# Two pairs of FFN chunks per phase as seven block products each, and TensorE in the written order from the third chunk on

## The chip, the cores and the metric

One core of one Trainium2 chip. The metric is the device time of one execution in microseconds (us); lower is better.

## What is computed

Two layers of a streaming encoder on a sequence of 256 tokens with model width 1024, everything in float32. Each layer is a half-step FFN, a mixer (attention and mLSTM heads) and another half-step FFN, each between two RMS norms. The change touches the FFN:

```python
def _swiglu(h, w_in, w_out):
    gate, up = jnp.split(h @ w_in, 2, axis=-1)
    return (jax.nn.silu(gate) * up) @ w_out
...
h = _swiglu(_rmsnorm(x, g[0]), ffn_w_in[l, 0], ffn_w_out[l, 0])
x = x + 0.5 * _rmsnorm(h, g[1])
```

Here `w_in` is 1024 x 5632 (gate and up side by side, 2816 each) and `w_out` is 2816 x 1024. A phase reads 33 MB of FFN weights, and there are four FFN phases and two mixers.

## The kernel before

**Precision.** TensorE multiplies fp32r numbers. Every weight and every activation is therefore split into a rounded high part and a low rest, and every product is three matmuls: high by high, high by low, low by high (`mm3`, L401, L402, L403).

**Tiling.** The hidden width 2816 is cut into 11 chunks of 256 (`NC_FF`), the tokens into two tiles of 128 (`NT`). For one chunk the first product ("I" below) takes, for each token tile, the two K halves (512 rows each, `kh`) of 512 columns: 256 gate columns and 256 up columns side by side in one PSUM bank of 512. That is 2 weight pieces and 48 matmuls of 128x512. The second product ("O") takes the chunk's 256 hidden columns to the 1024 outputs: 1 weight piece and 24 matmuls, added up in four `bk` banks over all chunks.

**Weights.** A piece is 128x2048 float32, 1 MB, loaded by one DMA of SP's queue into a raw tile `wr` (3 buffers, L282). It is worked on in two halves of 128x1024. ScalarE (ACT) makes the high part `wh` (L288), VectorE (DVE) the low part `wl` by subtracting it (L289). Halves lie in 7 buffers each of `wl` and `wh`, and in each run of ten halves three more come from the pool `k4` (`half_tiles`). So a half can be cast only when TensorE (PE) has finished with the half ten places before it.

**Between the two products.** ACT takes silu of the gate (L266), DVE makes `h` (L528), ACT writes `h` as 16-bit planes (L535), a transposing DMA of SP's queue turns it (`turned`, L537), DVE copies it together again (`hT`, L539), and ACT and DVE split it into `hh` (L550) and `hl` (L551). The last chunk is computed with weights and tokens exchanged (`in_turned`, `ffn_turned`), so that it needs no turning.

**Order.** The Python code writes I of chunk c, then O two chunks behind (`DEFER`). The framework's scheduler then decides where each instruction stands in its engine's queue; only from "ending" on (the last chunk's end of a phase, up to "running" of the next) does PE follow the written order. Each engine works through its queue in that fixed order. PSUM has 2 `pin`, 2 `ptr` and 4 `bk` banks.

Of the kernel before, what the change touches and what calls it, by code (L numbers as in the profile page):

```python
# [59 lines left out]
def _pack(inp):  # L60
# [9 lines left out]
    def ffn(at, l, f):  # L70
        a = w_in[l, f].reshape(2, 4, P, 2, NC_FF, 256)
        a = a.transpose(4, 0, 2, 1, 3, 5).reshape(NC_FF, 2, P, 2048)
        b = w_out[l, f].reshape(NC_FF, 2, P, D).transpose(0, 2, 1, 3).reshape(NC_FF, P, 2048)
        order = [a[0, 0], a[0, 1]]
        for c in range(1, NC_FF):
            order += [a[c, 0], a[c, 1], b[c - 1]]
        for piece in order + [b[NC_FF - 1]]:
# [54 lines left out]
class _Trunk:  # L132
# [144 lines left out]
    def begin_piece(self):  # L277

        nc, i = self.nc, self.piece_at
# [3 lines left out]
        js = iter(range(2))  # L283

        def part():
            j = next(js)
            lo, hi = self.half_tiles(i, j)
            ia = nc.scalar.activation(hi, raw[:, j], AF.Copy)  # L288
            iv = nc.vector.tensor_tensor(lo, raw[:, j], hi.bitcast(F32), op=ALU.subtract)  # L289
            for oa, ov in self.turns.pop(0) if self.turns else ():  # L290
                self.after(ia, [oa] if oa else [])
                self.after(iv, [ov] if ov else [])
# [237 lines left out]
    def ffn_planes(self, h):  # L530
# [8 lines left out]
        nc.vector.tensor_copy(hT.rearrange("p b n -> p (b n)").bitcast(U16).rearrange("p (n u) -> p u n", u=2),  # L539
                              turned.rearrange("p (u b) n -> p u (b n)", u=2))  # L540
# [46 lines left out]
    def ffn(self, pre, gi_post):  # L587
# [30 lines left out]
        po, pend = None, []  # L618
        if not xT:
# [12 lines left out]
            h = self.t2("h", (P, NT, 256))  # L632
            for t in range(NT):
                self.ffn_hidden(pins[t], r[t], h[:, t])
            h = self.ffn_planes(h)
            begin = 1
        else:
# [24 lines left out]
            h = self.ffn_planes(h)  # L662
            begin = 2
        for c in range(begin, NC_FF):
# [5 lines left out]
            if c < TURN:  # L670
                pins = [self.bank_pin() if c % 2 else self.bank_tr() for _ in range(NT)]
                for kh in range(2):
                    for t in range(NT):
                        in_piece(t, kh, pins[t], ws[kh])
# [582 lines left out]
```

## Time and profile before

| | |
|---|---|
| median of 3 runs | 961.61 us (961.54 to 962.01) |
| the profiled execution | 962.02 us |
| its span in the profile | 960.2 us |
| mean granted TensorE clock | 0.999 |

In the profile PE is the matrix engine, PEld its weight load, DVE VectorE, ACT ScalarE, POOL GpSimd, and SP the engine whose queue issues the DMAs. A row such as "L289 DVE TENSOR_TENSOR wl<-wr,wh 128x1024 ... x324 | 389.2, 1221 | 180.4 <-ACT wh L288 174.4" says: 324 instructions of line 289, 389.2 us busy in all, 1221 ns each, and 180.4 us of idle time of DVE just before them, 174.4 of it ended by the ACT instruction that wrote `wh`. In a timeline a row gives start, duration, engine, line and operation, and "x2" joins two neighbours.

### The profile page before, as it was taken

Reading aid. Unit: us, or ns where it says so; the run is one execution under the profiler, and the core shown is the slowest. Engines: PE = TensorE matmul, PEld = TensorE weight load, DVE = VectorE, ACT = ScalarE, POOL = GpSimd, SP = SyncE. Lnnn points to the kernel's source line nnn. Section 1 sums busy time; section 2 is a strip of 40 time slices with the busy share of each in tenths; the row PEclk is TensorE's granted clock in tenths of the full one; section 3 lists DMA queues with packets and bytes.
Section 4 is the critical chain, followed back from the end, with each engine's and each line's share of the span. In section 5 each row is a group of like instructions: output and inputs, shape, how many; then the busy total and the mean of one; then the engine's idle time right before and its main releaser. Section 6 shows DMA issues by size and latency. Waiting matters only on the chain.

```text
span 960.2 us, 12037 instructions
## 1 busy us (share of the span) xinstructions
PE 952.8 (99%) x4523; PEld 788.9 (82%) x4523; DVE 638.7 (67%) x945; ACT 571.2 (59%) x937; POOL 29.5 (3%) x55
## 2 busy tenths in 40 slices
PE   9999999999999999999999999999999999999997
PEld 7888888888888888888888888888888888888885
DVE  6765655689867766555687555566988676755553
ACT  8755554577856655454476555555778466555542
POOL 2000000000010000000000000000001000000000
PEclk9999999999999999999999999999999999999999
DMA  8996656236352975676458666653454257765621
GB/s 317 328 288 202 225 193 219 105 132 241 116 192 91 299 245 193 218 247 176 154 189 283 206 225 208 196 187 128 172 202 174 90 182 256 272 205 192 225 72 44
DMA packets 69879, 189.32 MB, mean 197 GB/s; under 512 B 45274, under 2 KB 46426, under 8 KB 49086
## 3 DMA queue, kind: packets, MB, share of 16 engines
q1 hardware_dynamic: 69246, 187.95, 58.0%
q8 instruction: 35, 0.57, 0.2%
q10 hardware_dynamic: 576, 0.61, 0.2%
q14 instruction: 22, 0.18, 0.1%
HBM read 177.01 MB, written 1.05 MB: 185 GB/s over the span
## 4 chain that ended last, share of the span: by engine, by line
PE 97%; DVE 1%; DMA 1%; ACT 0%; issue 0%; POOLq 0%; DVEq 0%; ACTq 0%
PE pin L401 13%; PE pin L402 13%; PE pin L403 13%; PE bk L401 10%; PE bk L402 10%; PE bk L403 10%; PE ptr L402 6%; PE ptr L403 6%; PE ptr L401 6%; PE pin L610 1%; PE ptr L610 1%; PE ptr L879 1%; PE ptr L427 1%; DMA wr<-in_w_dram 1%; PE bk L1094 1%; PE ptr L615 1%
## 5 line engine op out<-in xcount | busy, mean ns | idle before, releaser
L289 DVE TENSOR_TENSOR wl<-wr,wh 128x1024 fp32r<-128x1024 f32 x324 | 389.2, 1221 | 180.4 <-ACT wh L288 174.4
L288 ACT ACTIVATE wh<-wr 128x1024 fp32r<-128x1024 f32 x324 | 333.9, 1055 | 171.2 <-DMA wr<-in_w_dram 44.1
L401 PE MATMUL pin<-wh,both 128*128 128x512 f32 x560 | 221.2, 396 | 0.0
L403 PE MATMUL pin<-wh,both 128*128 128x512 f32 x560 | 218.3, 390 | 0.0
L402 PE MATMUL pin<-wl,both 128*128 128x512 f32 x560 | 218.2, 390 | 0.0
L401 PE MATMUL bk<-wh,hh 128*128 128x512 f32 x352 | 137.4, 390 | 0.1
L402 PE MATMUL bk<-wl,hh 128*128 128x512 f32 x352 | 137.0, 389 | 0.0
L403 PE MATMUL bk<-wh,hl 128*128 128x512 f32 x352 | 136.9, 389 | 0.0
L403 PEld LDWEIGHTS pin<-wh,both 128*128 128x128 f32 x560 | 105.1, 188 | 22.3
L401 PEld LDWEIGHTS pin<-wh,both 128*128 128x128 f32 x560 | 105.3, 188 | 22.0 <-issue 0.7
L402 PEld LDWEIGHTS pin<-wl,both 128*128 128x128 f32 x560 | 105.3, 188 | 20.6
L403 PE MATMUL ptr<-wh,both 128*128 128x512 f32 x256 | 99.4, 389 | 0.0
L402 PE MATMUL ptr<-wl,both 128*128 128x512 f32 x256 | 99.4, 389 | 0.0
L401 PE MATMUL ptr<-wh,both 128*128 128x512 f32 x256 | 98.9, 389 | 0.0
L401 PEld LDWEIGHTS bk<-wh,hh 128*128 128x128 f32 x352 | 66.1, 188 | 14.0 <-ACT hh L550 0.5
L403 PEld LDWEIGHTS bk<-wh,hl 128*128 128x128 f32 x352 | 66.1, 188 | 13.7
L402 PEld LDWEIGHTS bk<-wl,hh 128*128 128x128 f32 x352 | 66.1, 188 | 13.5
L539 DVE COPY hT<-turned 128x1024 uint16<-128x1024 uint16 x40 | 30.3, 757 | 41.9 <-DMA turned<-planes 41.5
L401 PEld LDWEIGHTS ptr<-wh,both 128*128 128x128 f32 x256 | 48.1, 188 | 10.0
L402 PEld LDWEIGHTS ptr<-wl,both 128*128 128x128 f32 x256 | 48.1, 188 | 10.0
L550 ACT ACTIVATE hh<-hT 128x256 fp32r<-128x256 f32 x80 | 28.9, 409 | 46.0 <-DVE hT L539 46.0
L403 PEld LDWEIGHTS ptr<-wh,both 128*128 128x128 f32 x256 | 48.1, 188 | 9.9
(210 smaller groups left out, 891.9 us busy)
## 6 DMA issues: line engine op xcount, KB each, us to landing
wr<-in_w_dram SPq DMA_DIRECT2D x162, 1024.0 KB, 5.2
gpost<-in_gpost_dram SPq DMA_DIRECT2D x6, 512.0 KB, 6.3
wr<-in_w_dram SPq DMA_DIRECT2D x2, 512.0 KB, 6.1
wr<-in_w_dram SPq DMA_DIRECT2D x3, 256.0 KB, 4.3
x<-in_x_dram SPq DMA_DIRECT2D x3, 256.0 KB, 4.4
turned<-planes SPq DMA_TRANSPOSE x40, 4.4
out_dram<-x SPq DMA_DIRECT2D x2, 256.0 KB, 2.1
x<-in_x_dram SPq DMA_DIRECT2D x2, 128.0 KB, 3.0
```

Of the source, the lines that this page charges most:

```text
L288: ia = nc.scalar.activation(hi, raw[:, j], AF.Copy)
L289: iv = nc.vector.tensor_tensor(lo, raw[:, j], hi.bitcast(F32), op=ALU.subtract)
L401: mm(ps, xh, wh, start=start, stop=False)
L402: mm(ps, xh, wl, start=False, stop=False)
L403: mm(ps, xl, wh, start=False, stop=stop)
L427: nc.tensor.transpose(ptr[:, k, :], x[:, (4 * hf + k) * P:(4 * hf + k + 1) * P], self.ident)
L539: nc.vector.tensor_copy(hT.rearrange("p b n -> p (b n)").bitcast(U16).rearrange("p (n u) -> p u n", u=2), turned.rearrange("p (u b) n -> p ...
L550: self.nc.scalar.activation(hh, h, AF.Copy)
L610: self.nc.tensor.matmul(b, self.cols(w[kh], k)[0][:, c], both[kh][:, k].rearrange("p i t -> p (i t)"), start=kh == 0 and k == 0, stop=Fals ...
L615: self.nc.tensor.matmul(b[:, 0:NT * P], self.cols(w[kh], k)[1][:, c], both[kh][:, k, 0:NT].rearrange("p i t -> p (i t)"), start=False, sto ...
L879: self.T(ptr[:, b, :], a[:, b * P:(b + 1) * P], self.tr.ident)
L1094: self.mm(pcs[c][:, h, :], self.qkT[0][rows, h0 + h, t * P:(t + 1) * P], self.qkT[1][rows, h0 + h, 0:nk], start=True, stop=True)
```

## The change

A phase now follows the list `STEPS`. `P4` and `P8` take the chunks 4 and 5, and 8 and 9, together as a 2 x 2 block product: token tile by K half, times K half by (gate or up of both chunks, 512 columns). In place of 8 products of 12 matmuls each (four k, three matmuls for each) there are 7 (Strassen's scheme in Winograd's form):

- `pair_blocks` loads the four weight blocks b11, b12, b22, b21 as pieces and makes their sums on DVE (L314, two 128x1024 halves to a sum: 8 additions for a pair), into the tile `run` (`wide`) or in place. Seven operands are split, in 14 halves, where four pieces made 8.
- `pair_tokens` makes the four sums of token blocks, once for each phase, at the first pair: on DVE ten rows of 128x512 (L344, L345, L346, L351, L352) and four low parts (L625), and four high parts on ACT (L624). Their tiles `sum` come from the same 5 buffers as `h`, `planes`, `turned` and `hT`.
- `pair` does the seven products on PE (`product`, L705) in the order P1 (b1), P5 (b4), P6 (b2), P7 (b3), P2 (onto b1), P3 (onto b4), P4 (onto b3), where b1 to b4 are the two `pin` and two `ptr` banks. P1 and P2 use tokens as they are; P5, P6, P7 and P3 use the four sums. In between, ACT copies b1 to `p1` (L717), and DVE makes `u` (L721) from b2 and p1, `v` from u, b3 (L723) and b4 (L724). P3 adds onto b4, so it comes after L724 has read b4. Then follow silu of 128x512, h0 (L728, L729), u (L732) and v (L734), and the two turned chunks.
- the copy to `hT` is moved from DVE to ACT (L609), the mixer's `qk` and `wt` lie in the tile `wide`, and the weights are packed in the new order of use.
- from the third chunk on PE stands under `manual_schedule`: its instructions keep the order in which `ffn` writes them. The other engines' order is still the scheduler's.

```diff
 BIG = -1.0e30
-DEFER = 3
-TURN = 10
+STEPS = "I2 O0 I3 O1 P4 O2 I6 O3 I7 O4 O5 P8 O6 O7 I10".split()
+END = (8, 9, 10)
...
+        for step in STEPS:
+            c = int(step[1:])
+            if step[0] == "P":
+                order += [n[kh, g, :, :, c:c + 2].reshape(P, 2048) for kh, g in ((0, 0), (0, 1), (1, 1), (1, 0))]
+            else:
+                order += [a[c, 0], a[c, 1]] if step[0] == "I" else [b[c]]
...
-    for _n in ("nat", "ra", "rb", "rv", "tmp", "y", "so", "xg", "h", "planes", "turned", "hT"):
+    for _n in ("nat", "ra", "rb", "rv", "tmp", "y", "so", "xg", "h", "planes", "turned", "hT", "u", "v", "sum"):
...
-        self.qk = self.ded.tile([P, 4, S], F32, name="qk")
-        self.wt = self.ded.tile([P, NT, 2, 2, P], F32, name="wt")
...
+        raw, js = self.fetch(), iter(range(2))
+        return lambda: self.halved(raw[:, next(js)])
+
+    def fetch(self):
+
         nc, i = self.nc, self.piece_at
         self.piece_at += 1
         raw = self.raw_tile(i)
         self.load = nc.sync.dma_start(raw.rearrange("p a b -> p (a b)"), self.a["w"][i])
...
+        return raw
+
+    def halved(self, raw):
+
+        nc = self.nc
+        lo, hi = self.half_tiles()
+        ia = nc.scalar.activation(hi, raw, AF.Copy)
+        iv = nc.vector.tensor_tensor(lo, raw, hi.bitcast(F32), op=ALU.subtract)
+        for oa, ov in self.turns.pop(0) if self.turns else ():
+            self.after(ia, [oa] if oa else [])
+            self.after(iv, [ov] if ov else [])
+        return hi, lo
+
+    def wide(self):
+        return self.k4.tile([P, 2, 1024], F32, tag="wide", bufs=1, name=self.name("wide"))
+
+    def pair_blocks(self):
+
+        def split(raw):
+            return [self.halved(raw[:, j]) for j in range(2)]
+
+        def add(out, a, b):
+            for j in range(2):
+                self.nc.vector.tensor_tensor(out[:, j], a[:, j], b[:, j], op=ALU.add)
+
+        b11, b12 = self.fetch(), self.fetch()
+        w = {"P1": split(b11)}
+        run = self.wide()
+        add(run, b11, b12)
+        w["P5"] = split(run)
+        b22 = self.fetch()
+        add(run, run, b22)
+        w["P6"] = split(run)
+        add(b12, b12, b22)
+        w["P7"] = split(b12)
+        b21 = self.fetch()
+        w["P2"] = split(b21)
+        w["P3"] = split(b22)
+        add(run, run, b21)
+        w["P4"] = split(run)
+        return w
+
+    def pair_tokens(self, both):
+
+        tt = self.nc.vector.tensor_tensor
+        tiles = [self.tr.tile([P, 4, 2 * NT, P], F32R, tag="both", name=self.name("both")) for _ in range(2)]
+
+        def a(kh, t, lo):
+            return both[kh][:, :, lo * NT + t, :].bitcast(F32)
+
+        def apart(x, y):
+            s, low = (self.t2("sum", (P, 4, P)) for _ in range(2))
+            tt(s, a(*x, 0), a(*y, 0), op=ALU.subtract)
+            tt(low, a(*x, 1), a(*y, 1), op=ALU.subtract)
+            tt(s, s, low, op=ALU.add)
+            return s
+
+        def less(x, y):
+            s = self.t2("sum", (P, 4, P))
+            tt(s, a(*x, 0), y, op=ALU.subtract)
+            tt(s, s, a(*x, 1), op=ALU.add)
+            return s
+
+        def split(i, s):
+            hi, lo = (tiles[i // 2][:, :, n + i % 2, :] for n in (0, NT))
+            self.ffn_hilo(s, hi, lo)
             return hi, lo
 
...
 
         nc = self.nc
         planes = self.t2("planes", (P, 2, 512), U16)
-        nc.scalar.activation(planes, h.rearrange("p t j -> p (t j)").bitcast(U16).rearrange("p (n u) -> p u n", u=2), AF.Copy)
+        nc.scalar.activation(planes, h.bitcast(U16).rearrange("p (n u) -> p u n", u=2), AF.Copy)
         turned = self.t2("turned", (P, 8, P), U16)
         nc.sync.dma_start_transpose(turned, planes.rearrange("p u n -> p (u n)"))
-        hT = self.t2("hT", (P, 4, P))
-        nc.vector.tensor_copy(hT.rearrange("p b n -> p (b n)").bitcast(U16).rearrange("p (n u) -> p u n", u=2),
-                              turned.rearrange("p (u b) n -> p u (b n)", u=2))
+        hT = self.t2("hT", (P, 2, 2, P))
+        nc.scalar.activation(hT.rearrange("p a b n -> p (a b n)").bitcast(U16).rearrange("p (n u) -> p u n", u=2),
+                             turned.rearrange("p (u b) n -> p u (b n)", u=2), AF.Copy)
+        return hT
+
+    def ffn_split(self, hs):
+
         ops = [self.ffn_operand() for _ in range(NT)]
-        for t in range(NT):
-            self.ffn_hilo(hT[:, 2 * t:2 * t + 2], *ops[t])
-        return [[tuple(v[:, k] for v in ops[t]) for k in range(2)] for t in range(NT)]
+        for h, op in zip(hs, ops):
+            self.ffn_hilo(h, *op)
+        return [[tuple(v[:, k] for v in op) for k in range(2)] for op in ops]
 
...
-        po, pend = None, []
+        def ready(h):
+            hT = self.ffn_planes(h.rearrange("p t j -> p (t j)"))
+            return self.ffn_split([hT[:, t] for t in range(NT)])
+
+        def chunk(c, pins):
+            h = self.t2("h", (P, NT, 256))
+            for t in range(NT):
+                self.ffn_hidden(pins[t], r[t], h[:, t])
+            hs[c] = ready(h)
+
+        def product(b, x, w, new):
+            for k in range(4):
+                for n, (st, mv) in enumerate(((x[0], 0), (x[0], 1), (x[1], 0))):
+                    self.nc.tensor.matmul(b, st[:, k, :], self.cols(w, k)[mv], start=new and k == n == 0,
+                                          stop=k == 3 and n == 2, skip_group_check=True)
+
+        def pair(c):
+
+            tt, stt = self.nc.vector.tensor_tensor, self.nc.vector.scalar_tensor_tensor
+            w = self.pair_blocks()
+            b1, b2, b3, b4 = self.bank_pin(), self.bank_pin(), self.bank_tr(), self.bank_tr()
+            s1, s2, s3, s4 = sums
+            product(b1, xT[0][0], w["P1"], True)
+            p1 = self.t2("p1")
+            self.nc.scalar.activation(p1, b1, AF.Copy)
+            product(b4, s1, w["P5"], True)
+            product(b2, s2, w["P6"], True)
+            u, v, h0, sil = self.t2("u"), self.t2("v"), self.t2("h"), self.t2("sil")
+            tt(u, b2, p1, op=ALU.subtract)
+            product(b3, s3, w["P7"], True)
+            tt(v, u, b3, op=ALU.subtract)
+            tt(v, v, b4, op=ALU.add)
+            product(b1, xT[0][1], w["P2"], False)
+            self.func(sil, b1, AF.Silu, scale=r[0])
+            product(b4, s4, w["P3"], False)
+            tt(h0, b4, u, op=ALU.add)
+            stt(h0, h0, r[0], sil, op0=ALU.mult, op1=ALU.mult)
+            hT = [self.ffn_planes(h0)]
+            product(b3, xT[1][1], w["P4"], False)
+            tt(u, b3, u, op=ALU.subtract)
+            self.func(u, u, AF.Silu, scale=r[1])
+            stt(v, v, r[1], u, op0=ALU.mult, op1=ALU.mult)
+            hT.append(self.ffn_planes(v))
+            for j in range(2):
+                hs[c + j] = self.ffn_split([h[:, j] for h in hT])
+
+        hs, po = {}, []
...
+            hs[1] = ready(h)
+        with self.tc.manual_schedule(engines={mybir.EngineType.PE}):
+            both, sums, swap = list(self.both), None, 0
+            for step in STEPS[:-1]:
+                c = int(step[1:])
+                if step[0] == "P":
+                    sums = sums or self.pair_tokens(both)
+                    pair(c)
+                elif step[0] == "I":
+                    if c == 3:
+                        g = self.load_gpost(gi_post)
+                        yield "middle"
+                    ws = [self.piece(), self.piece()]
+                    pins = [self.bank_pin() if swap else self.bank_tr() for _ in range(NT)]
+                    swap = 1 - swap
+                    for kh in range(2):
+                        for t in range(NT):
+                            in_piece(t, kh, pins[t], ws[kh])
+                    chunk(c, pins)
+                else:
+                    if not po:
+                        po = [[self.bank_bk() for _ in range(2)] for _ in range(NT)]
+                    wo = self.piece()
+                    for t in range(NT):
+                        out_part(c, t, hs[c], wo)
             ws = [self.piece(), self.piece()]
-            pend.append((c - 1, h, self.piece()))
-            if c == 3:
-                g = self.load_gpost(gi_post)
-                yield "middle"
...
+            rows = self.token_scales(r)
+            last = [self.piece() for _ in END[:-1]]
+            banks = [[self.bank_pin() for _ in range(2)], [self.bank_tr() for _ in range(2)]]
+            in_turned(banks, ws, both)
 
         yield "ending"
...
+        two = tr.wide()
+        self.qk = two[:, 0].rearrange("p (b s) -> p b s", b=4)
+        self.wt = two[:, 1].rearrange("p (t a b j) -> p t a b j", t=NT, a=2, b=2)
```

**How it moves instructions.** In each place the second FFN of the first layer is shown. VectorE before the change, around chunk 4's first product (its pieces are `wr_60` and `wr_61`; `wr_62` is the second product of chunk 3, `hT_401` the turned chunk 2, `h_413` the hidden tile of chunk 3):

```order
L289 TENSOR_TENSOR wl_60_0_3334<-wr_60_3332,wh_60_0_3335 128x1024
L289 TENSOR_TENSOR wl_60_1_3338<-wr_60_3332,wh_60_1_3339 128x1024
L289 TENSOR_TENSOR wl_61_1_3348<-wr_61_3342,wh_61_1_3349 128x1024
L539 COPY hT_401_3167<-turned_400_3165 128x2x512
L289 TENSOR_TENSOR wl_61_0_3344<-wr_61_3342,wh_61_0_3345 128x1024
L551 TENSOR_TENSOR hl_403_3170<-hT_401_3167,hh_402_3169 128x256
L551 TENSOR_TENSOR hl_405_3172<-hT_401_3167,hh_404_3171 128x256
L528 SCALAR_TENSOR_TENSOR h_413_3287<-pin_411_3237,rs1_360_2854,sil_414_3288 128x256
L289 TENSOR_TENSOR wl_62_0_3354<-wr_62_3352,wh_62_0_3355 128x1024
L528 SCALAR_TENSOR_TENSOR h_413_3287<-pin_412_3238,rs1_373_2941,sil_415_3291 128x256
L289 TENSOR_TENSOR wl_63_0_3459<-wr_63_3457,wh_63_0_3460 128x1024
```

After at most four splits a small row follows. VectorE after the change, at the end of the first pair's operands (`wr_62` is here b21, `wr_61` b22, `hT_683` the turned chunk 3, `sum_694` the sum s1, `both_692` the split sums s1 and s2):

```order
L297 TENSOR_TENSOR wl_717_3469<-wr_62_3467,wh_718_3470 128x1024
L297 TENSOR_TENSOR wl_719_3473<-wr_62_3467,wh_720_3474 128x1024
L344 TENSOR_TENSOR sum_694_3398<-both_574_2866,both_577_2876 128x512
L345 TENSOR_TENSOR sum_695_3399<-both_574_2866,both_577_2876 128x512
L297 TENSOR_TENSOR wl_721_3477<-wr_61_3445,wh_722_3478 128x1024
L346 TENSOR_TENSOR sum_694_3398<-sum_694_3398,sum_695_3399 128x512
L297 TENSOR_TENSOR wl_723_3481<-wr_61_3445,wh_724_3482 128x1024
L625 TENSOR_TENSOR hl_685_3355<-hT_683_3352,hh_684_3354 128x256
L625 TENSOR_TENSOR hl_687_3357<-hT_683_3352,hh_686_3356 128x256
L351 TENSOR_TENSOR sum_696_3405<-both_574_2866,sum_694_3398 128x512
L625 TENSOR_TENSOR both_692_3396<-sum_694_3398,both_692_3396 128x4x128
```

The splits of the pair stand together, ahead of the token sums; the low part of s1 (the last row) stands behind both halves of the operand of P3 (`wl_721`, `wl_723`). VectorE a few rows on, up to the second v, which frees bank b4 (`ptr_732`) for P3 (`wide_704` is the operand of P4, `wr_63` the second product of chunk 2, `wr_64` chunk 6):

```order
L297 TENSOR_TENSOR wl_727_3491<-wide_704_3434,wh_728_3492 128x1024
L297 TENSOR_TENSOR wl_752_3628<-wr_63_3626,wh_753_3629 128x1024
L721 TENSOR_TENSOR u_734_3537<-pin_730_3496,p1_733_3511 128x512
L297 TENSOR_TENSOR wl_754_3632<-wr_63_3626,wh_755_3633 128x1024
L297 TENSOR_TENSOR wl_756_3662<-wr_64_3660,wh_757_3663 128x1024
L723 TENSOR_TENSOR v_735_3538<-u_734_3537,ptr_731_3497 128x512
L297 TENSOR_TENSOR wl_758_3666<-wr_64_3660,wh_759_3667 128x1024
L724 TENSOR_TENSOR v_735_3538<-v_735_3538,ptr_732_3498 128x512
```

Splits of later steps stand ahead of the two rows of v. TensorE before the change, from the end of chunk 1's second product (`bk_409`) to the start of chunk 4 (`both_345` is the tokens' first K half):

```order
L402 MATMUL bk_409_3180<-wl_56_1_3102,hh_392_3070 128x512
L403 MATMUL bk_409_3180<-wh_56_1_3103,hl_393_3071 128x512
L401 MATMUL ptr_423_3362<-wh_60_0_3335,both_345_2794 128x512
L402 MATMUL ptr_423_3362<-wl_60_0_3334,both_345_2794 128x512
L403 MATMUL ptr_423_3362<-wh_60_0_3335,both_345_2794 128x512
L401 MATMUL ptr_423_3362<-wh_60_0_3335,both_345_2794 128x512
```

TensorE after the change, from the end of P1 to the start of P5 (`pin_729` is b1, `ptr_732` is b4, `wh_706` and `wl_705` the operand b11 + b12):

```order
L705 MATMUL pin_729_3495<-wh_703_3431,both_574_2866 128x512 x2
L705 MATMUL pin_729_3495<-wl_702_3430,both_574_2866 128x512
L705 MATMUL pin_729_3495<-wh_703_3431,both_574_2866 128x512
L705 MATMUL ptr_732_3498<-wh_706_3438,both_692_3396 128x512
L705 MATMUL ptr_732_3498<-wl_705_3437,both_692_3396 128x512
```

The first product of the pair takes the tokens as they were (`both_574`); the second, P5, takes the sum s1 in `both_692`, which VectorE writes in the row shown above.

More of the change, by code (lines that the diff above doesn't have):

```diff
@@ L70, in ffn @@
     def ffn(at, l, f):
-        a = w_in[l, f].reshape(2, 4, P, 2, NC_FF, 256)
-        a = a.transpose(4, 0, 2, 1, 3, 5).reshape(NC_FF, 2, P, 2048)
+        n = w_in[l, f].reshape(2, 4, P, 2, NC_FF, 256).transpose(0, 3, 2, 1, 4, 5)
+        a = n.transpose(4, 0, 2, 3, 1, 5).reshape(NC_FF, 2, P, 2048)
         b = w_out[l, f].reshape(NC_FF, 2, P, D).transpose(0, 2, 1, 3).reshape(NC_FF, P, 2048)
[L74 to L77, printed above, removed]
+        order = [a[0, 0], a[0, 1], a[1, 0], a[1, 1]]
+        for step in STEPS:
[4 more added lines that the diff above has]
+                order += [a[c, 0], a[c, 1]] if step[0] == "I" else [b[c]]
+        for piece in order + [b[c] for c in END]:
             w[at] = piece
@@ L282, in begin_piece @@
         self.load = nc.sync.dma_start(raw.rearrange("p a b -> p (a b)"), self.a["w"][i])
[L283 to L292, printed above, removed]
-            return hi, lo
@@ new lines, in pair_tokens @@
+    def pair_tokens(self, both):
[17 more added lines that the diff above has]
+            self.ffn_hilo(s, hi, lo)
+            return hi, lo
+        s1 = apart((0, 1), (1, 1))
+        x1 = split(0, s1)
+        s2 = less((0, 0), s1)
+        x2 = split(1, s2)
+        x4 = split(3, less((1, 0), s2))
+        return x1, x2, split(2, apart((0, 0), (0, 1))), x4
@@ L299, in half_tiles @@
+    def half_tiles(self):
         pools = (self.k4, "k4", self.k4, "k4") if self.lend and self.halves % 10 in (2, 5, 8) else (self.wl, "wl", self.wh, "wh")
         self.halves += 1
-        return [pools[n].tile([P, 1024], F32R, tag=pools[n + 1], name=f"{nm}_{i}_{j}") for n, nm in ((0, "wl"), (2, "wh"))]
+        return [pools[n].tile([P, 1024], F32R, tag=pools[n + 1], name=self.name(nm)) for n, nm in ((0, "wl"), (2, "wh"))]
     def raw_tile(self, i):
@@ L631, in ffn @@
                 r.append(self.rsqrt_sum(ss, EPS))
[L632 to L636, printed above, removed]
+            chunk(0, pins)
+            w1 = [self.piece(), self.piece()]
+            pins = [self.bank_pin() for _ in range(NT)]
+            for kh in range(2):
+                for t in range(NT):
+                    in_piece(t, kh, pins[t], w1[kh])
+            chunk(1, pins)
         else:
@@ L654, in ffn @@
             self.ffn_hidden(pb, r[1], h[:, 1])
-            pend = [(0, self.ffn_planes(h), self.piece())]
+            hs[0] = ready(h)
             pb1 = self.bank_pin()
@@ L661, in ffn @@
             self.ffn_hidden(pb1, r[1], h[:, 1])
-            h = self.ffn_planes(h)
-            begin = 2
-        for c in range(begin, NC_FF):
-            ws = [self.piece(), self.piece()]
-            pend.append((c - 1, h, self.piece()))
-            if c == 3:
-                g = self.load_gpost(gi_post)
-                yield "middle"
[L670 to L674, printed above, removed]
-                h = self.t2("h", (P, NT, 256))
-                for t in range(NT):
-                    self.ffn_hidden(pins[t], r[t], h[:, t])
-                h = self.ffn_planes(h)
-            else:
-                rows, both = self.token_scales(r), list(self.both)
-                banks = [[self.bank_pin() for _ in range(2)], [self.bank_tr() for _ in range(2)]]
-                in_turned(banks, ws, both)
-                break
-            if len(pend) == DEFER - 1:
-                if po is None:
-                    po = [[self.bank_bk() for _ in range(2)] for _ in range(NT)]
-                cc, hc, wo = pend.pop(0)
-                for t in range(NT):
-                    out_part(cc, t, hc, wo)
@@ L691, in ffn @@
         yield "ending"
-        pend.append((c, self.ffn_turned(banks, rows), self.piece()))
-        for p in pend:
-            out_part(p[0], 0, *p[1:])
+        hs[END[-1]] = self.ffn_turned(banks, rows)
+        last.append(self.piece())
+        for c, wo in zip(END, last):
+            out_part(c, 0, hs[c], wo)
         yield "done", po[0], g
-        for p in pend[:-1]:
-            out_part(p[0], 1, *p[1:])
+        for c, wo in zip(END[:-1], last):
+            out_part(c, 1, hs[c], wo)
@@ L698, in ffn @@
         yield "next"
-        out_part(pend[-1][0], 1, *pend[-1][1:])
+        out_part(END[-1], 1, hs[END[-1]], last[-1])
         yield "done", po[1], g
@@ L914, in conv_silu @@
         tr, conv = self.tr, self.conved
[L915 to L916 removed]
+        tr.func(self.qk, conv, AF.Silu)
+        self.q, self.kT = self.qk[:, 0:2, :], self.qk[:, 2:4, :]
         tr.table("exp_and_others", self.rv)
```

12 lines of the change are left out of this document (5 added, 7 removed).

## The prediction

> **What bounds the kernel now.** First the page's busy times, then the chain that ended last:
>
> ```profile
> span 960.2 us, 12037 instructions
> PE 952.8 (99%) x4523; PEld 788.9 (82%) x4523; DVE 638.7 (67%) x945; ACT 571.2 (59%) x937; POOL 29.5 (3%) x55
> PE 97%; DVE 1%; DMA 1%; ACT 0%; issue 0%; POOLq 0%; DVEq 0%; ACTq 0%
> ```
>
> The matmul queue has next to no holes and the chain is PE. The windows of an FFN phase (the second of layer 0; after the stretch come busy time and count of PE, PEld, DVE, ACT and POOL, then the granted clock) say the same of the stage that is changed:
>
> ```profile
> 340.00:376.00 36.00, 36.00 (x161) 29.81 (x160) 22.61 (x29) 21.30 (x28) 0.00 (x0) 1.00 0.67 229
> 376.00:412.00 36.00, 36.00 (x161) 29.81 (x160) 20.83 (x24) 19.06 (x24) 0.00 (x0) 1.00 0.62 213
> ```
>
> PE is busy through, DVE 58 to 63%. The rows of all waits show why DVE idles and what ACT waits for:
>
> ```profile
> DVE wl L289 <- ACT wh L288: 174.4, 136, 3.3
> DVE hT L539 <- DMA turned<-planes: 41.5, 27, 4.2
> ACT wh L288 <- PE bk L403: 33.8, 18, 2.7
> ```
>
> DVE waits for ACT's casts, ACT for PE to give a half tile free. The split halves run ten ahead at most, and PE sets the pace. The reserve is short: ten halves are two and a half chunks' pieces, so a stretch in which DVE has more to do than PE cannot be prepared far ahead.
>
> **What PE saves.** The PE timeline gives the pace; the first of 24 matmuls of a second product and the first one behind it are
>
> ```profile
> 105.49 0.39 PE L401 MATMUL bk<-wh,hh 128*128 128x512 f32 x1
> ...
> 110.93 0.39 PE L401 MATMUL pin<-wh,both 128*128 128x512 f32 x1
> ```
>
> so 24 take 5.44 us, one 0.2267 (the 0.39 is its duration, they overlap), one I 10.88, one product of 12 2.72. Each pair saves 12 matmuls, 8 pairs save 96: 96 x 0.2267 = 21.8 us, 5.44 for a phase. With PE still full the profiled 962.0 would become 940.2.
>
> **What DVE gets.** For each pair six more splits and eight additions of 128x1024; at the first pair of a phase ten sums and four low parts of 128x512 as well; the evacuation is of 128x512 in place of 128x256. Additions in this form the trace doesn't show; the split is a subtraction of the same shape and gets the same price, and the 512-wide ones go by L433 and the rows from PSUM by L472. Rows from the groups by form and from the DVE timeline:
>
> ```profile
> L289 DVE TENSOR_TENSOR wl<-wr,wh 128x1024 fp32r<-128x1024 f32 x324 | 389.2, 1221 | 180.4 <-ACT wh L288 174.4 <-PE ptr L558 2.9 <-PE ptr L615 2.2
> L288 ACT ACTIVATE wh<-wr 128x1024 fp32r<-128x1024 f32 x324 | 333.9, 1055 | 171.2 <-DMA wr<-in_w_dram 44.1 <-PE bk L403 33.8 <-PE bk L402 25.1
> L433 DVE TENSOR_TENSOR both<-xg,both 128x512 fp32r<-128x512 f32 x20 | 12.9, 689 | 1.0
> L472 DVE TENSOR_TENSOR tmp<-bk,gpost 128x512 f32<-128x512 f32 x24 | 16.4, 685 | 19.0 <-ACT junk L468 19.0
> L539 DVE COPY hT<-turned 128x1024 uint16<-128x1024 uint16 x40 | 30.3, 757 | 41.9 <-DMA turned<-planes 41.5
> L551 DVE TENSOR_TENSOR hl<-hT,hh 128x256 fp32r<-128x256 f32 x80 | 30.1, 418 | 1.0 <-ACT hh L550 1.0
> L528 DVE SCALAR_TENSOR_TENSOR h<-pin,rs,sil 128x256 f32<-128x256 f32 x46 | 22.0, 479 | 10.8 <-ACT sil L266 10.8
> 16.82 2.36 DVE L289 TENSOR_TENSOR wl<-wr,wh 128x1024 fp32r<-128x1024 f32 x2 [0.79 <-ACT wh L288]
> 19.10 0.48 DVE L528 SCALAR_TENSOR_TENSOR h<-bk,rs,sil 128x256 f32<-128x256 f32 x1
> 19.49 1.22 DVE L289 TENSOR_TENSOR wl<-wr,wh 128x1024 fp32r<-128x1024 f32 x1
> 33.31 0.75 DVE L551 TENSOR_TENSOR hl<-hT,hh 128x256 fp32r<-128x256 f32 x2
> 187.29 1.29 DVE L433 TENSOR_TENSOR both<-xg,both 128x512 fp32r<-128x512 f32 x2
> ```
>
> Neighbours on DVE overlap a little, so there are two prices. By the mean: 1.22 for 1024 wide, 0.69 for 512, 0.42 for hl, 0.48 for h. By the pitch, the second one's share of a joined row: 2.36 - 1.22 = 1.14, 1.29 - 0.69 = 0.60, 0.75 - 0.42 = 0.33, and 19.49 - 19.10 = 0.39. I take the pitch, since in a full queue it is what counts; the means are the upper bound.
>
> Over the whole kernel DVE gets 8 x 14 x 1.22 + 4 x 14 x 0.69 + some 23 for the evacuation, and loses the 40 hT copies: about 640 + 137 + 39 + 23 - 30 = 809 us. That fits into 940. It does not fit where it falls.
>
> **The first pair's stretch**, the second FFN of layer 0. PE's order from the end of I2 to P3 is O0, I3, O1, P1, P5, P6, P7, P2: 5.44 + 10.88 + 5.44 + 5 x 2.72 = 35.4 us. In the same time DVE must get from the split of P1's first half to the second v, since P3 adds to the bank that this v reads. DVE's queue holds 53 rows there: 26 of 1024 width (the pair's 14 splits, its 8 additions, and four splits of O2 and I6), 17 of 512 width (14 for the token sums, u, v, v), 6 hl, 4 h. By pitch 26 x 1.14 + 17 x 0.60 + 6 x 0.33 + 4 x 0.39 = 43.4 us, by means 47.9. It cannot begin early: the cast of P1's first half needs the tile of the half ten before it, that is the first half of I2's second piece, which PE leaves 6 matmuls (1.36 us) before I2's end; with the cast (1.06) DVE starts 0.3 before I2's end. So PE waits at least 43.4 - 0.3 - 35.4 = 7.7 us ahead of P3, by means 12.2.
>
> Part of the wait comes at P5 already, which needs s1's low part: up to there DVE has 20 wide rows, 6 hl, 4 h and 5 of 512, 22.8 + 2.0 + 1.6 + 3.0 = 29.4 - 0.3 = 29.1 us, and PE gets there after O0, I3, O1 and P1, in 24.5: 4.6 us. A second chain gives nearly the same: wl_723 stands ahead of that low part, and its cast needs the half ten places before, P1's second, so after P1's end come 1.06 + 1.14 + 2 x 0.33 + 2 x 0.60 = 4.1 us.
>
> The same count in the other phases: the third and fourth FFN have one wide row more and start 0.5 before I2's end, 44.5 - 0.5 - 35.4 = 8.7 each (13.2 by means). The first FFN goes from O0's end, 23 wide, 4 hl, 2 h and 17 of 512: 26.2 + 1.3 + 0.8 + 10.2 + 0.2 = 38.7, less PE's 29.9, is 8.8 (12.7). Sum of four: 33.9 us, by means 51.3.
>
> **ACT with the hT copy.** The copy waited for its transposing DMA on DVE; now the wait stands in ACT's queue ahead of casts (hT_683 ahead of wh_724, the cast of the second chain above), two in each stretch. Before, these waits were 41.5 us over 40 copies, 1.0 each. Some of it falls where casts would wait for PE anyway, so I take 1.5 of the 2.1 us: 6 us for four phases, with bounds 0 and 8.3. ACT's own work I take as no limit: in the stretch it has 18 casts (19 us) where DVE has 26 wide rows (29.6), and copies, planes and activations beside them stay under the rest.
>
> **The second pair** needs no sums. Its first half needs the tile of O3's first half, so DVE's stretch goes from O3's end to v: 24 wide rows, 5 hl, 2 h and u, v, v, by pitch 27.4 + 1.7 + 0.8 + 1.8 = 31.7 us, against I7, O4, O5 and five products of PE, 35.4. It fits. Only v's own chain remains (P7's end, then the cast and split ahead of the second v, and v: 1.06 + 1.14 + 0.60 = 2.8 against P2's 2.72), 0.1 to 0.9 for a pair; I take 0.5, 2 us in all.
>
> **Nothing for the rest.** The fixed PE order removes no wait, since PE hardly had any. qk and wt in a shared tile are needed in the mixer alone. The pieces are as many as before; a pair's loads wait for raw tiles that DVE frees, and take by the page
>
> ```profile
> wr<-in_w_dram SPq DMA_DIRECT2D x162, 1024.0 KB, 5.2
> ```
>
> 5.2 us. b22 takes the tile of O1's piece, whose last split stands just ahead of P1's; up to b22's first addition DVE has 6.0 us of rows (4 wide, 2 h, 2 hl), so it hardly waits; for b21 there is twice that.
>
> **Sum.** 962.0 - 21.8 + 33.9 + 6 + 2 = 982.1; the profiled run is 0.4 above the median of the runs shown, so 982 within the rounding. Low end of the forecast's own range: pitches alone, 962.0 - 21.8 + 33.9 = 974. High end: 962.0 - 21.8 + 51.3 + 8.3 + 2 = 1002.
>
> **Rivals.** A: PE stays the bound and the time is 940. For it speak the 99%, and DVE's 809 us of 940. It decides if DVE does the 53 rows within 35.4 us, 0.67 a row, and no wide row of the page is under 1.1; against it stands also that the rows are in a fixed queue. By the Trainium skill, page "Perfetto Trace Analysis", section "Identifying the Most-Contended Engine", the engine of the highest occupancy is to be improved first, which is PE here and would give this case's 940; the trace agrees on the engine for before alone. Chance 0.10.
>
> B: the waits also cost clock. The only cold matmuls in the trace are the first ones of the program:
>
> ```profile
> L390 PE MATMUL bk<-const-bfloat16-1.0 128*128 128x512 bf16 x8 | 3.9, 617 | 0.8 <-PEq L1247 0.8
> L401 PE MATMUL bk<-wh,hh 128*128 128x512 f32 x352 | 137.4, 390 | 0.1
> ```
>
> 617 ns against 390. If the 12 products after a long wait ran so, 12 x 0.227 = 2.7 us for a wait. Behind P5 this is covered, since DVE then has 14 us more to v and PE 10.9; behind the wait at P3 it is not: four phases, 10.9 us, 993; with the means for DVE above 1002. The Trainium skill, "TensorE: Matmul & The Clock Gate", Part 1, states that an idle window of about 3.4 us halves the clock until PE was busy as long again. No wait of this trace is long enough to show it; by that rule the waits at P5 (4.6 us) are over the bound and those at P3 (3 us) close to it. Chance 0.12.
>
> C: only the wait at P5 counts, since the rows behind it are done under P5 to P2. It decides if the 24 rows after s1's low part take 10.9 us; by pitch they take 14. Then 962.0 - 21.8 + 4 x 4.6 + 2 = 960.6, within about 3 of the old time. Chance 0.10, of which 0.04 faster, 0.04 the same, 0.02 slower.
>
> **Numbers.** The forecast has 0.68. A measurement tells about 0.2% (1.9 us) from no change. Faster: A and part of C, 0.14; same 0.04; slower: forecast, B and the rest of C, 0.82. The range from 958 to 1002 leaves out A and the upper half of B.
>
> **What would show it.** PE waits at the first pair of every phase, for DVE's low part of s1 (L625) ahead of P5 (some 4 to 7 us) and for v (L724) ahead of P3 (some 3 to 6), and nearly nothing at the second; PE's busy time falls to about 931; DVE is busy through from I2's end to v and has about 809 us. It is wrong if PE has no such waits, if they lie at other places (weights by DMA, ACT's casts, P8), or if DVE's additions take another time than its splits.

## The result, and the profile after

| | before | changed |
|---|---|---|
| median | 961.81 us (961.54 to 962.80, 4 runs) | 1004.38 us (1002.96 to 1005.70, 4 runs) |
| profiled execution, its span | 962.02, 960.2 us | 1002.96, 1001.2 us |

The ratio is 1.044 (95% interval 1.0422 to 1.0459): slower, as forecast, but by 42.6 us where 20 were forecast, and 2 us above the stated range. One execution of all that follow, of the first run with the early sums in a place of their own, took 3357 us and is left out of its median. The page of the changed kernel and its list of PE's waits (engine, tile and line that waited, engine, tile and line waited for; us in all, times, longest):

```profile
span 1001.2 us, 12171 instructions
PE 946.8 (95%) x4427; PEld 777.4 (78%) x4427; DVE 790.8 (79%) x1097; ACT 679.0 (68%) x1033; POOL 28.4 (3%) x55
PEclk9989999999999998999999799999999999899999
```

```profile
PE ptr L705 <- ACT both L624: 27.4, 4, 9.8
PE ptr L705 <- DVE v L724: 11.4, 8, 3.0
PE bk L471 <- ACT hh L624: 4.7, 3, 1.7
PE ptr L705 <- DVE both L625: 1.6, 1, 1.6
PE ptr L1008 <- DVE ra L1193: 1.2, 1, 1.2
PE ptr L1008 <- DVE y L1271: 0.8, 1, 0.8
```

The 96 matmuls are gone (4523 to 4427). PE is idle 54.4 us where it was 7.4, 47.0 more, and the list says where: 29.0 at P5 (once in each FFN phase), 11.4 at P3 (twice), 4.7 at the last second product of three phases, 2.0 in a mixer. PE's busy time fell by 6.0 in place of 21.8, so its matmuls took 15.8 us longer. 47.0 + 15.8 - 21.8 = 41.0, the whole difference of the spans.

Some 12 of the 15.8 us are a halved clock: behind five of the waits 55 matmuls in all keep a distance of about 0.43 us or more, in place of 0.227. The rest falls on the first and last matmuls at the waits, which have no neighbour to overlap with. Windows of the first pair in the second FFN (P1 and the wait; P5; P6 and P7; P2 and the wait; the granted clock is the number after POOL's):

```profile
368.50:375.40 6.90, 2.93 (x13) 2.08 (x12) 6.90 (x8) 6.61 (x9) 0.00 (x0) 1.00 0.81 258
375.40:382.30 6.90, 5.21 (x13) 3.82 (x14) 6.87 (x13) 2.47 (x5) 0.00 (x0) 0.60 0.63 236
382.30:388.40 6.10, 6.10 (x26) 4.95 (x25) 6.10 (x7) 4.61 (x5) 0.00 (x0) 0.89 0.00 0
388.40:392.00 3.60, 2.85 (x13) 2.04 (x11) 3.60 (x6) 2.84 (x4) 0.00 (x0) 1.00 0.69 218
```

DVE (the third busy time with its count) is busy in 23.47 of these 23.50 us: it is the bound of this stretch, and behind the wait PE runs P5 at a clock of 0.60. PE's own rows there:

```profile
375.47 0.50 PE L705 MATMUL ptr<-wh,both 128*128 128x512 f32 x1 [4.04 <-ACT both L624]
375.81 0.40 PE L705 MATMUL ptr<-wl,both 128*128 128x512 f32 x1
377.82 1.22 PE L705 MATMUL ptr<-wh,both 128*128 128x512 f32 x2 [1.61 <-DVE both L625]
378.84 0.63 PE L705 MATMUL ptr<-wl,both 128*128 128x512 f32 x1
379.26 1.05 PE L705 MATMUL ptr<-wh,both 128*128 128x512 f32 x2
...
392.04 0.50 PE L705 MATMUL ptr<-wh,both 128*128 128x512 f32 x1 [0.79 <-DVE v L724]
```

P5's first matmul waits for the high part of s1, the second for the low part, then they follow each other at 0.43 us in place of 0.227. P3 starts at 392.04, when the second v has been written:

```profile
391.31 0.68 DVE L724 TENSOR_TENSOR v<-v,ptr 128x512 f32<-128x512 f32 x1
```

So two accounts fit the books: DVE's queue sets P3, and the slow matmuls ahead of it only fill a wait (theory Q), or the lost clock itself costs its 16 us (theory C, the prediction's rival B). A third, O, lays the time on the rest of the change: written order, packing, ACT's copy.

### The profile page after: what moved, and what is told of

It reads as the page before. It is cut to its first block, busy times and chain, and to the rows that moved or that the text cites. A ratio compares the mean times of both kernels' runs of the same rounds, so it can differ in the third digit from the quotient of the medians.

```text
span 1001.2 us, 12171 instructions
## 1 busy us (share of the span) xinstructions
PE 946.8 (95%) x4427; PEld 777.4 (78%) x4427; DVE 790.8 (79%) x1097; ACT 679.0 (68%) x1033; POOL 28.4 (3%) x55
## 3 DMA queue, kind: packets, MB, share of 16 engines
HBM read 177.01 MB, written 1.05 MB: 178 GB/s over the span
## 4 chain that ended last, share of the span: by engine, by line
PE 70%; DVE 14%; ACT 8%; DMA 5%; issue 3%; SPq 0%; POOLq 0%; DVEq 0%; ACTq 0%
PE ptr L705 8%; PE bk L471 8%; PE bk L473 8%; PE bk L472 8%; PE pin L471 7%; PE pin L473 7%; PE pin L472 7%; DVE wl L297 6%; PE pin L705 4%; ACT wh L296 3%; DMA turned<-planes 3%; PE ptr L471 2%; PE ptr L473 2%; PE ptr L472 2%; DMA wr<-in_w_dram 2%
## 5 line engine op out<-in xcount | busy, mean ns | idle before, releaser
L471 PE MATMUL pin<-wh,both 128*128 128x512 f32 x432 | 171.4, 398 | 0.0
L473 PE MATMUL pin<-wh,both 128*128 128x512 f32 x432 | 168.5, 390 | 0.0
L472 PE MATMUL pin<-wl,both 128*128 128x512 f32 x432 | 168.4, 390 | 0.0
L705 PE MATMUL ptr<-wh,both 128*128 128x512 f32 x256 | 92.3, 428 | 40.4 <-ACT both L624 27.4
L705 PEld LDWEIGHTS ptr<-wh,both 128*128 128x128 f32 x256 | 52.4, 206 | 57.7 <-ACT both L624 29.1
L473 PEld LDWEIGHTS pin<-wh,both 128*128 128x128 f32 x432 | 81.1, 188 | 17.4
L471 PEld LDWEIGHTS pin<-wh,both 128*128 128x128 f32 x432 | 81.3, 188 | 17.0 <-issue 0.7
L472 PEld LDWEIGHTS pin<-wl,both 128*128 128x128 f32 x432 | 81.2, 188 | 15.6
L609 ACT ACTIVATE hT<-turned 128x1024 uint16<-128x1024 uint16 x40 | 54.7, 1369 | 32.9 <-DMA turned<-planes 32.8
L296 ACT ACTIVATE wh<-wide 128x1024 fp32r<-128x1024 f32 x48 | 50.4, 1055 | 22.7 <-DVE wide L314 14.1
L705 PE MATMUL pin<-wh,both 128*128 128x512 f32 x192 | 63.7, 393 | 0.0
L297 DVE TENSOR_TENSOR wl<-wide,wh 128x1024 fp32r<-128x1024 f32 x48 | 57.9, 1218 | 0.7
L705 PE MATMUL ptr<-wl,both 128*128 128x512 f32 x128 | 53.8, 420 | 0.0
L471 PE MATMUL ptr<-wh,both 128*128 128x512 f32 x128 | 49.8, 389 | 0.0
```

The lines of the kernel that those rows point to most:

```text
L296: ia = nc.scalar.activation(hi, raw, AF.Copy)
L297: iv = nc.vector.tensor_tensor(lo, raw, hi.bitcast(F32), op=ALU.subtract)
L471: mm(ps, xh, wh, start=start, stop=False)
L472: mm(ps, xh, wl, start=False, stop=False)
L473: mm(ps, xl, wh, start=False, stop=stop)
L609: nc.scalar.activation(hT.rearrange("p a b n -> p (a b n)").bitcast(U16).rearrange("p (n u) -> p u n", u=2), turned.rearrange("p (u b) n - ...
```

## The experiments

The first four set these apart; each is timed against the kernel before on its own chip (961.4 to 962.3 us there).

**PE kept busy in the wait.**

```diff
+            if c == 4:
+                for _ in range(32):
+                    self.nc.tensor.matmul(b4, one.broadcast_to([P, P]), one.broadcast_to([P, 512]), start=True, stop=True)
             product(b4, s1, w["P5"], True)
```

> 32 bf16 matmuls of 128x512 on constants are put into bank b4 between P1 and P5 of the first pair, 7.3 us at 0.2267 each, thrown away by P5's start. They fill the wait at P5 and keep the clock up. Theory Q: P3 is still held by VectorE's queue, so what the clock gains ahead of P3 becomes wait, and only the cold matmuls behind P3 go: 1000 to 1005 us. Theory C (the half clock after the waits costs its 16 us): 988 to 993 us.

Measured: 1008.7 us (1005.5 to 1012.0), ratio 1.0488 (1.0460 to 1.0516). In the second FFN the wait at P5 is gone and the clock never falls, yet P3 starts no earlier after P1 (the trace lacks the record of one of the 32):

```profile
372.21 6.95 PE L721 MATMUL ptr<-const-bfloat16-1.0 128*128 128x512 bf16 x31
378.81 0.58 PE L705 MATMUL ptr<-wh,both 128*128 128x512 f32 x1
...
393.33 0.50 PE L705 MATMUL ptr<-wh,both 128*128 128x512 f32 x1 [1.05 <-DVE v L728]
```

```profile
376.00:382.00 6.00, 6.00 (x29) 3.85 (x27) 5.97 (x11) 2.33 (x4) 0.00 (x0) 1.00 0.82 314
```

From P1 to P3 it takes 393.33 - 369.26 = 24.1 us, without the filling 392.04 - 368.55 = 23.5. In this stretch theory C falls for the matmuls ahead of P3: DVE is busy in 5.97 of the 6.00 us shown, and what the clock gains PE waits, 1.66 us in P7 for the low part of s3 and 1.05 ahead of P3.

The total says less. It lies 4 us above Q's 1000 to 1005, and from P1 to P3 the four phases take 4.2 us more than in the changed kernel. In the first and third FFN the filling is too short: 2.66 and 2.21 us of the wait at P5 are left, with slow matmuls behind them. And the edit moved rows of DVE as well: in the second and third FFN one split more stands ahead of the low part of s3, and P7 now waits 1.5 to 2.0 us for that row in all four.

**No pairs**, with the rest of the change.

```diff
-STEPS = "I2 O0 I3 O1 P4 O2 I6 O3 I7 O4 O5 P8 O6 O7 I10".split()
+STEPS = "I2 O0 I3 O1 I4 O2 I5 O3 I6 O4 I7 O5 I8 O6 I9 O7 I10".split()
```

> No pair: all chunks as I and O, the rest of the change (PE in written order, hT copy on ACT, qk and wt in the shared tile) stays. Theory Q: no stretch is short of VectorE, 960 to 965 us. Theory O: 975 or more.

Measured: 966.7 us (966.6 to 967.5), ratio 1.0053 (1.0038 to 1.0068), neither's number quite. The rest of the change costs 4.9 us, and PE's waits give 4.5 of it, at the same place as in the changed kernel:

```profile
PE bk L471 <- ACT hh L624: 4.5, 3, 1.5
```

**The hT copy back on DVE** (`nc.vector.tensor_copy` in `ffn_planes`).

> The hT copy goes back from ACT to VectorE, all else as changed. Theory Q: VectorE gets two to three rows of 0.67 us in each first stretch and the wait for the transposing DMA besides: 1004 + 4 x (1.3 to 4) = 1009 to 1020 us. Theory O, with ACT's copy as the cause: 985 to 998 us.

Measured: 1008.5 us (1007.1 to 1008.9), ratio 1.0483 (1.0467 to 1.0499): 4 us slower than the changed kernel, so the copy's move to ACT was no cause; the loss is half a us below what Q gave.

**Token sums early.** `pair_tokens` is called ahead of I2, and its rows are bound, one or two at a time, ahead of the next splits:

```diff
-            both, sums, swap = list(self.both), None, 0
+            both, swap = list(self.both), 0
+            sums = self.pair_tokens(both)
...
+        for n, row in enumerate((1, 2, 4, 5, 7, 8, 10, 11, 12, 13)):
+            self.turns[n] = list(self.turns[n]) + [(None, rows[row])]
```

> The fourteen VectorE rows of the token sums are made between the splits of chunk 2, O0 and chunk 3, ahead of the first pair's stretch; nothing else is changed. Theory Q (VectorE's queue sets when P5 and P3 start): the stretch loses 14 x 0.60 = 8.4 us of its 43.4, so PE waits 0 to 3 us ahead of P3 in each phase instead of 10 to 15, and no wait is long enough to lose clock; 962.0 - 21.8 + 4 x (0 to 3) + 3 for the second pair + 5 for the second products = 948 to 962. Theory O (the written PE order, the new packing or ACT's copy cost the time, the sums do not): stays above 990.

Measured: 1031.7 us (1031.2 to 1033.0), ratio 1.0729 (1.0711 to 1.0747). Q's number is missed by 70. The wait at P5 is gone, as Q says, but there are two others:

```profile
PE ptr L714 <- DVE v L733: 31.3, 8, 7.0
PE ptr L481 <- DVE wl L297: 20.6, 4, 8.5
```

The second is new: PE waits at I2 for its splits, which I had bound behind the first sums, and the row of a sum waits in turn for ACT's work on planes, with which `sum` shares its buffers:

```profile
348.15 0.69 DVE L339 TENSOR_TENSOR sum<-both,both 128x512 f32<-128x512 f32 x1 [0.53 <-ACT planes L614]
348.76 1.22 DVE L297 TENSOR_TENSOR wl<-wr,wh 128x1024 fp32r<-128x1024 f32 x1
```

The experiment had brought in its own wait. The next has it without: the sums lie in `wide`, idle until the first pair, and bind only splits from O0 on.

```diff
+        two = self.wide()
+        f = [two[:, i // 2, i % 2 * 512:i % 2 * 512 + 512].rearrange("p (k t) -> p k t", k=4) for i in range(4)]
...
+        for n, row in enumerate((None, None, None, None, 2, 4, 6, 8, 10, 11, 12, 13)):
```

> As the run with early sums, with its two faults mended: the sums lie in the tile 'wide', which is idle until the first pair, in place of the buffers shared with h, planes, turned and hT, and their rows are bound only to the splits from O0 on, none ahead of chunk 2's. Theory Q (VectorE's queue sets P5 and P3): the first stretch loses 14 x 0.60 = 8.4 us, PE waits 0 to 3 us ahead of P3 in each phase: 966.7 (no pairs) - 21.8 + 4 x (0 to 3) + 3 = 948 to 960. Theory S (the phase has no free VectorE time anywhere, rows that are moved come back as waits at another place): 985 or more.

Measured: 983.8 us (982.7 to 983.8, three executions), ratio 1.0223 (1.0206 to 1.0241): 20 us better than the changed kernel, and still 24 above Q's upper number. The fourth execution, the profiled one, is the one of 3357 us, so the kernel was run once more for a profile:

> The kernel with the early sums in their own place once more, for an undisturbed profile. Theory V: its 984 in place of 948 to 960 comes from v's place on VectorE: with the sums gone the scheduler put v behind three or four splits of later steps, whose half tiles PE frees only in P7 and P2, so that v waits for P2 and P3 for v. Then P5 has no long wait, P3 waits 3 to 8 us in each first pair for the second v, and the splits just ahead of v wait for ACT's casts, those for PE. Theory S (no free VectorE time): waits at P5, P1 or at chunk 2, with VectorE busy through.

Measured: 981.0 us (one run). P5 has no wait left; P3 has:

```profile
PE ptr L722 <- DVE v L741: 20.3, 8, 6.1
PE bk L488 <- ACT hh L641: 4.5, 3, 1.5
PE pin L722 <- DVE wl L297: 2.3, 2, 1.3
```

DVE around the two v in the second FFN:

```profile
373.80 0.68 DVE L738 TENSOR_TENSOR u<-pin,p 128x512 f32<-128x512 f32 x1
374.40 3.49 DVE L297 TENSOR_TENSOR wl<-wr,wh 128x1024 fp32r<-128x1024 f32 x3
377.80 0.68 DVE L740 TENSOR_TENSOR v<-u,ptr 128x512 f32<-128x512 f32 x1
378.40 3.49 DVE L297 TENSOR_TENSOR wl<-wr,wh 128x1024 fp32r<-128x1024 f32 x3
381.81 0.68 DVE L741 TENSOR_TENSOR v<-v,ptr 128x512 f32<-128x512 f32 x1
```

P2 began at 373.53, so P7 had ended. Six splits of O2 and I6 stand between u and the second v: 6.8 us that nobody needs yet, ahead of the row that P3 needs. V is right about the place; these splits wait for no tile, though, as V had it, they are only in front. And here the clock does count: PE is busy 942.4 us, 11 over its full-speed 931, since all four waits at a first P3 have 5 to 12 slow matmuls behind them, and no wait of PE follows there that could hide them.

**P4 ahead of P3** (its operand's split too), so that v has a product more of cover.

```diff
+            product(b3, xT[1][1], w["P4"], False)
             product(b4, s4, w["P3"], False)
...
-            product(b3, xT[1][1], w["P4"], False)
```

In the changed kernel:

> The changed kernel with P4 ahead of P3 on PE, and P4's operand split ahead of P3's; the sums stay where they were. Theory Q: P5's waits (29 us) stay, and of the waits at P3 (11.4 us) most goes: 991 to 998. Theory V as well. If the sums' place is not what P5 waits for, below 980.

Measured: 988.1 us (986.3 to 991.7), ratio 1.0272 (1.0249 to 1.0294). 16 us go, 3 more than Q had at most; P3's waits are gone, P5's stay:

```profile
PE ptr L705 <- ACT both L624: 26.0, 4, 8.8
PE bk L471 <- ACT hh L624: 4.7, 3, 1.7
PE ptr L705 <- DVE both L625: 1.6, 2, 1.1
```

With the early sums:

> Early sums in their own place and P4 ahead of P3, without the change at the phases' ends. Theory V: P3's wait goes, 952.7 of the fast version + 4.5 for the ends = 955 to 959. If the end's order was what made the difference of 31 us: 975 to 984.

Measured: 956.6 us (956.2 to 958.8), ratio 0.9945 (0.9929 to 0.9962), as V had it, and faster than before the change. Neither edit alone is enough: 20 to 23 us for the sums, 16 for the order, 48 for both.

**The ends of the phases.** In the order of the changed program 12 matmuls of chunk 8's second product stand amid chunk 10's first product; before, they stood behind it, where they cover the evacuation of chunk 10. Bound behind it again:

```diff
+                    if c == END[0] and t == 0:
+                        self.after(i, [self.turned_last])
```

> No pairs, all of the rest of the change, but the first second product of the end stands behind all of chunk 10's first product. The 966.7 without pairs had three waits of 1.5 us there: 962 to 963, the time before the change. If the written order costs elsewhere: 966 to 967.

Measured without pairs: 962.2 us (961.5 to 963.0, 10 runs), ratio 0.9998 (0.9989 to 1.0008). All that the rest of the change had cost was this order. With everything together:

> The run before, and two waits of the rest taken away: P4 stands ahead of P3 on PE (its operand's splits too), so that v's chain has a product more to end in, and the first second product of the end (chunk 8, first token tile) stands behind the whole of chunk 10's first product, as cover for its evacuation. Theory Q: the second pair's 4 x 0.8 and the ends' 4.5 us go: 3 to 8 us below the run before, 943 to 954. Theory S: within 2 us of the run before.

Measured: **952.7 us** (951.6 to 953.0), ratio 0.9901 (0.9884 to 0.9917): 9 us faster than before the change. Its longest waits:

```profile
PE ptr L725 <- DVE v L743: 3.8, 2, 1.9
PE ptr L725 <- DVE v L744: 2.0, 2, 1.1
```

It was expected 3 to 8 us below the early sums alone and came out 31 below: P4's place alone was worth 24 to 27 (956.6 against 981.0 and 983.8), since P3's waits there also cost clock.

**GpSimd in DVE's place.** First the pair's additions (`add` on `nc.gpsimd`):

> The eight 128x1024 additions of a pair are done by GpSimd in place of VectorE; the sums stay where they are. Theory Q: the first stretch loses 8 x 1.14 = 9.1 us of VectorE, and if GpSimd adds a half within 4 us the waits go as with the sums: 948 to 965. If GpSimd is slower than that (its time for this is not in the traces), the operands come late and the time is above 1004. Theory S: 985 or more, with GpSimd's additions short.

Measured: 1055.4 us (1054.0 to 1058.6), ratio 1.0977 (1.0955 to 1.0999). Groups by form:

```profile
L314 POOL TENSOR_TENSOR wide<-wide,wr 128x1024 f32<-128x1024 f32 x32 | 86.8, 2723 | 28.1 <-DVE wl L297 28.1
L297 DVE TENSOR_TENSOR wl<-wide,wh 128x1024 fp32r<-128x1024 f32 x48 | 98.6, 2070 | 20.7 <-ACT wh L296 20.7
L296 ACT ACTIVATE wh<-wide 128x1024 fp32r<-128x1024 f32 x48 | 50.2, 1057 | 61.0 <-POOL wide L314 51.3
```

Then the sums' ten rows, in `wide`, early:

> The ten rows of the token sums on GpSimd, in the tile 'wide', made as soon as the tokens are there; the four low parts on VectorE as before. Theory Q: the stretch loses 6.0 to 8.4 us: 948 to 962. Theory S: near that too, since VectorE loses the rows for good; it differs from the moved rows only if those stay slow.

Measured: 1008.4 us (1004.5 to 1008.8), ratio 1.0474 (1.0454 to 1.0494). Both miss. An addition on GpSimd is under the 4 us that I had allowed, but six of them follow each other on one tile, ACT waits 51 us for them, and DVE's own rows get longer beside them: a split of `wide` takes 2070 ns on the mean in place of 1218. Taken apart by time, the 27 splits of `wide` that overlap an addition of GpSimd take 2735 ns and the other 21 take 1214; of the splits of `wr` 24 overlap one, at 2256 ns, and the other 300 take 1219. So DVE's busy time rose from 790.8 to 825.5 us, although 76 us of additions had left it. The second kernel still has P3 ahead of P4 and waits 21.0 us for v; what part of its rest is GpSimd's was not separated.

## Why the prediction was right and wrong

**The saving on PE** was right: 96 matmuls, 21.8 us; busy time at full clock would be 931, as forecast. With the slow matmuls it is 946.8; the kernel of 952.7 us, with the same 4427 matmuls, has 934.5.

**The bound** was right: DVE in the first pair's stretch, PE waiting at P5 and P3, next to nothing at P8. PE waits at the places that were named, but not in the shares: P5 5.6 to 9.8 us in place of 4 to 7, P3 0.8 to 3.0 in place of 3 to 6. Most of the wait at P5 is put down to ACT's high part of s1, which is cast as soon as DVE has the sum (the rows of the third FFN below), so DVE's queue is behind it all the same. DVE's busy time is 790.8 where 809 by the means was named. The price of an addition was right too (1216 ns, the split's). So was the pitch: in the second FFN the rows from P1's first split

```profile
346.73 1.23 DVE L297 TENSOR_TENSOR wl<-wr,wh 128x1024 fp32r<-128x1024 f32 x1 [0.63 <-ACT wh L296]
349.32 2.36 DVE L314 TENSOR_TENSOR wide<-wr,wr 128x1024 f32<-128x1024 f32 x2 [1.37 <-DMA wr<-in_w_dram]
```

to the end of v at 391.99 took 45.3 us against 43.4 counted, and 1.37 of the rest is the one wait for b12's DMA.

**The size of the stretch** was too small. From P1's start to P3's, less 13.6 of products, PE lost 15.1, 9.9, 13.5 and 11.0 us in the four phases, 49.5 together; "Sum of four: 33.9 us" and the 6 for ACT make 39.9. Two steps of the count failed.

The first is the count of the first FFN, "23 wide" rows from O0's end. O0 ends at 45.60, where PE starts I3, and P1's first split follows behind:

```profile
45.60 0.39 PE L471 MATMUL pin<-wh,both 128*128 128x512 f32 x1
46.33 0.43 DVE L216 TENSOR_TENSOR lamp<-lamv 128x256 f32<-128x256 f32 x1 [1.24 <-DMA lamv<-in_lam_dram]
46.67 1.22 DVE L297 TENSOR_TENSOR wl<-wr,wh 128x1024 fp32r<-128x1024 f32 x1
```

From there to the end of v at 90.53 the trace has 27 wide rows, 19 splits and 8 additions, with no idle time between them. Four rows too few, at 1.14, are 4.6 us of the 6.3 by which this phase was short. Another 1.4 are the mixer's constants, which fall into the stretch and were left out of the count: 0.7 of DVE's wait for their DMA lies behind O0's end, and two small rows are 0.7.

The second is that loads were held to be no matter. The prediction looked at b22 and b21; DVE waits for b12, 1.37, 0.96 and 0.71 us in the other three FFNs.

Most of what is left falls to ACT, for which the 6 us stood. In the third FFN DVE itself stood still for the turned tile, 2.16 us, ahead of the sums; ACT's cast of s1 then waits for DVE's sum:

```profile
565.44 1.34 ACT L609 ACTIVATE hT<-turned 128x1024 uint16<-128x1024 uint16 x1 [2.50 <-DMA turned<-planes]
...
568.33 0.63 ACT L624 ACTIVATE both<-sum 128x512 fp32r<-128x512 f32 x1 [0.79 <-DVE sum L346]
```

```profile
567.27 0.43 DVE L625 TENSOR_TENSOR hl<-hT,hh 128x256 fp32r<-128x256 f32 x1 [2.16 <-ACT hh L624]
```

In the fourth FFN a cast costs 0.94, and P1's first split comes 0.2, 1.1 and 0.2 us later than counted in the second to fourth. That is 4.6 us with the 2.16, so the term for ACT was not too small. Some 2 us more are rows that take a little longer than their pitch.

**"Nothing for the rest. The fixed PE order removes no wait"** failed. It removed none and added one at the end of three phases, 4.7 us; without the pairs the same order costs 4.9, and with 12 matmuls put back nothing. I had looked at the order around the pairs and not at the phases' ends. This is the largest term that the prediction put at nothing; with it the forecast's high end would have been above the measured time.

**The second pair** was 2 and is 4.1: waits of 0.81, 0.81, 0.66 and 0.66 and a slow end and start of the matmuls around each. In the first mixer PE waits 2.0 us for DVE (ra, y), which no pair explains; that the run without pairs does not have them is all that is known.

**Rival B, the clock**, came true as an event and not as a cause at P5: "Behind P5 this is covered, since DVE then has 14 us more to v" is what the filled wait shows. Behind P3 it counts: in the third FFN eight matmuls or so follow at 0.43, which with the slow starts in the other phases is some 2 us that the sum had at nothing; with the early sums it is 8 us (942.4 busy against 934.2 with P4 first). Reading PE's books alone, waits of 40.4 at P5 and P3 against the forecast's 41.9 and 15.8 of slow matmuls on top, one would have taken the clock for the missing 16.

**Rival A** (940) failed for this order of the rows. With the same work, the sums moved out of the stretch and v covered, the kernel comes within 13 us of it. **Rival C** failed: P3 did wait.

Forecast terms: -21.8 + 39.9 + 2 = 20.1. Measured: -21.8 + 49.5 + 2.1 (clock behind P3) + 4.1 + 4.7 + 2.0 (mixer) = 40.6 of the 40.9 between the two profiled runs. So the mechanism was right, and the sum was short in the first stretch (9.6), at the ends of the phases (4.7), in the second pair and behind P3 (2.1 each) and in the mixer (2.0).

## What to carry to other kernels

Where a change trades work of the bound engine for work of a half idle one, count the second engine's queue from the earliest point at which buffers let it start to the row that the first engine waits for, other parts' rows in between included; the average share (67% for DVE here) did not show it. Then look at what stands ahead of the row that frees a bank: moving one product, fourteen small rows and the order at the ends turned 43 us lost into 9 gained. A slow clock behind a wait is a cost only if nothing else would have held the next step, and a few thrown-away matmuls can test that, in a stretch where they fill the whole wait and move nothing else.
